# A three-block network in fp32-like products: value projections 512 features wide, and the modulations' partition sums on column tiles

## The chip, the cores and the metric

The kernel runs on one core of one Trainium2 chip. The metric is device time of one execution in microseconds (us); lower is better. A core has five engines with a queue each: TensorE for matrix products (PE in the profile, its weight loads PEld), VectorE (DVE), ScalarE (ACT), GpSimd (POOL) and SyncE (SP), which here only issues transfers. Each executes its own queue in order, and semaphores join them. A change counts here as faster or slower if it moves the time by over 0.5%.

## The reference

One sequence of 512 tokens with 1024 features goes through three blocks, here 0, 1 and 2. Each block is modulated: a vector `c` gives six vectors of 1024 numbers (shift, scale and gate for its two halves), that is 12 groups of 512 columns.

```
c_act = silu(c)
mod = c_act @ w_ada[l] + b_ada[l]
sh1, sc1, g1, sh2, sc2, g2 = split(mod, 6)
h = rms_norm(x, norm1_g[l]) * (1.0 + sc1) + sh1
x = x + g1 * mixer(h, ...)
h2 = rms_norm(x, norm2_g[l]) * (1.0 + sc2) + sh2
gate, up = split(h2 @ w_ffn_in[l], 2)
x = x + g2 * ((silu(gate) * up) @ w_ffn_out[l])
```

Block 0's mixer is dilated attention next to a gated delta rule. The mixer of the other two merges three bidirectional gated linear attentions (a, b, c) of four heads each. Every attention has a value projection `h @ w` of 512 tokens by 512 features: one in block 0 (va), three in each other block (cv, av, bv), seven in all.

## The kernel before

`T` = 512 tokens, `P` = 128 partitions, `KT` = 8 tiles of 128 features. The normed input `h` lies with features on partitions, as a high and a low part (`hh`, `hl`, in fp32r), and so does each strip of weights (`whi`, `wlo`): a product is three matmuls, high by high, high by low, low by high (`mm3`, lines 119 to 123). `strip` (104) loads 512 KB of weights on SP's queue into `raw` (2 buffers), casts it on ACT to `whi` (line 101) and subtracts on DVE to `wlo` (line 102; 3 buffers of each), with a raised priority so that it runs ahead. Most projections (`proj`, 125) hold a weight tile fixed and let 512 tokens move: 24 matmuls into one PSUM bank.

The value projections are the other way round, `proj_tok` (183): tokens must come out on partitions, so a 128x128 tile of `h` is held fixed and weights move. A call does 256 of the 512 features, with two strips of 512 rows by 256 columns held through the call. For each of 4 token tiles it issues 8 x 3 matmuls that move 256 columns (lines 193 to 195), 96 in all, into half a bank; two banks of tag `mm` hold the result. Two calls make one projection, so there are 14 calls and 1344 such matmuls. `dst` then takes both banks: a copy on ACT for va, a split on ACT and DVE for cv and av (lines 101 and 102), and for bv a copy, a mean and a subtraction first (1201 to 1207). PSUM has 3 banks of tag `mm` (projections) and 5 of tag `mx` (everything else).

The modulations are not matrix products. `ada` (283) multiplies 128 x 512 tiles of `w_ada` by a column of `c_act` and adds them up on DVE into `acc` (305, 307). What is left, the sum over 128 partitions, is `ada_sum` (317), one group of 512 columns at a time. Block 0 (`li` = 0; groups 4 to 11, during the first mixer) does it with one fp32 matmul against a column of ones, which the profile records as two passes. Blocks 1 and 2 (all 12 groups, during the feed-forward of the block ahead) first split `acc` on ACT and DVE and then use two fp32r matmuls. Both are line 325. A sum is traced where the next group begins. The row is scaled on ACT (326), written to DRAM (327), read back (332) and transposed (340). Block 0's `acc` has two buffers, and its weight tiles (`araw`) two buffers of 256 KB.

`Dense` holds such work as a list of items with a cost each. The chains of the mixers call `fill(us)` at every step, which issues items until their cost is covered; `proj_tok`'s items are 2 x 5.2 us each, before the change. In the mixers the chain `c_decay` (1223), then `scan` (1067) with its copies `kt` (1085) and small matmuls (1104, 1123), is traced ahead of the value projection that fills its waits. The framework's scheduler orders each engine's queue at build time, by priority (the order of tracing, unless raised) and its own estimate of durations, and inserts every wait; a tile takes any free buffer of its tag. The modulations of block 0's first norm, which the change doesn't touch, already put fp32 matmuls of 32 columns on four column tiles (`ada_first`, line 387).

## Time and profile before

| what | value |
|---|---|
| median of 3 runs | 2854.15 us (2843.81 to 2860.08) |
| the profiled execution, span | 2841.0 us |
| PE busy | 2774.7 us (98%), 17518 matmuls |
| PEld busy | 2234.6 us (79%) |
| DVE busy | 1721.8 us (61%) |
| ACT busy | 1172.0 us (41%) |
| transfers | 330.66 MB, mean 116 GB/s |
| mean granted TensorE clock | 0.994 |

The span runs from the first to the last instruction of the profiled execution, which lies 13 us below the median of the runs and 3 us below the fastest. Matmuls are pipelined: a record lasts from its start to a modelled end and overlaps the next one, so what a matmul costs is read from one start to the next, not from its duration. A granted clock of 1.00 is 2.4 GHz, 0.50 is 1.2 GHz.

### The profile page before, as it was taken

What the parts mean: (1) busy time and instruction counts of PE and PEld (TensorE: products, weight loads), DVE (VectorE), ACT (ScalarE), POOL (GpSimd) and SP (SyncE); (2) the same over time, 40 slices, a digit from 0 to 9 for tenths busy, and PEclk for the clock granted to TensorE, in tenths of its full rate; (3) what the DMA queues carried; (4) which work ended last, traced back from release to release, by engine and by line L of the source; (5) the groups of instructions that cost most, each with busy time, mean ns of one, the idle gap of its engine ahead of it and who ended that gap; (6) DMA issues with size and microseconds to landing.
All of it is one profiled execution on the core that took longest, in us unless ns stands there. A gap on an engine that the chain in (4) does not pass through costs nothing.

```text
span 2841.0 us, 42612 instructions
## 1 busy us (share of the span) xinstructions
PE 2774.7 (98%) x17518; PEld 2234.6 (79%) x17518; DVE 1721.8 (61%) x2690; ACT 1172.0 (41%) x1796; POOL 41.7 (1%) x79
## 2 busy tenths in 40 slices
PE   7999999999999999999999999999999999999998
PEld 4786678878888887787887888877877888888887
DVE  4677646747377767756466563567777665533334
ACT  4643324222255655444343222465454443422223
POOL 0011000000000000100000000000000000000000
PEclk9999999999999999999999999999999999999999
DMA  7454524646232222332446463322223324333332
GB/s 259 126 157 117 156 87 144 228 150 215 84 110 62 68 72 68 101 93 83 133 134 210 153 224 93 103 66 68 68 75 90 99 80 130 89 97 96 92 94 82
DMA packets 471315, 330.66 MB, mean 116 GB/s; under 512 B 15447, under 2 KB 426223, under 8 KB 469584
## 3 DMA queue, kind: packets, MB, share of 16 engines
q1 hardware_dynamic: 468176, 320.51, 37.2%
q0 software_dynamic: 2944, 7.43, 0.9%
q8 instruction: 138, 2.26, 0.3%
q14 instruction: 57, 0.47, 0.1%
HBM read 312.55 MB, written 13.24 MB: 115 GB/s over the span
## 4 chain that ended last, share of the span: by engine, by line
PE 89%; DVE 4%; ACT 3%; DMA 2%; issue 1%; SPq 1%; POOL 0%; ACTq 0%; DVEq 0%; POOLq 0%
PE mm L121 22%; PE mm L122 22%; PE mm L123 22%; PE mx L121 3%; PE mx L122 3%; PE mx L123 3%; PE mm L193 1%; PE mm L195 1%; PE mm L194 1%; PE mx L1104 1%; PE mx L1123 1%; ACT whi L101 1%; PE mx L325 1%; PE mx L940 1%; DVE R L1154 1%
## 5 line engine op out<-in xcount | busy, mean ns | idle before, releaser
L121 PE MATMUL mm<-hh,whi 128*128 128x512 f32 (+1 forms) x2248 | 873.0, 391 | 12.4 <-ACT hh L487 9.0
L122 PE MATMUL mm<-hl,whi 128*128 128x512 f32 (+1 forms) x2248 | 876.9, 391 | 2.5 <-DVE hl L488 1.8
L101 ACT CAST whi<-raw 128x1024 fp32r<-128x1024 f32 (+2 forms) x451 | 438.3, 973 | 1068.6 <-PE mm L122 737.9
L123 PE MATMUL mm<-hh,wlo 128*128 128x512 f32 (+1 forms) x2248 | 874.0, 390 | 0.0
L102 DVE TENSOR_TENSOR wlo<-raw,whi 128x1024 fp32r<-128x1024 f32 (+2 forms) x451 | 507.4, 1126 | 361.5 <-ACT whi L101 350.0
L121 PEld LDWEIGHTS mm<-hh,whi 128*128 128x128 f32 x2248 | 419.6, 188 | 113.6 <-ACT hh L487 12.0
L122 PEld LDWEIGHTS mm<-hl,whi 128*128 128x128 f32 x2248 | 422.6, 188 | 102.5 <-DVE hl L488 6.0
L123 PEld LDWEIGHTS mm<-hh,wlo 128*128 128x128 f32 x2248 | 422.5, 188 | 93.4 <-issue 0.8
L122 PE MATMUL mm<-hid,whi 128*128 128x512 f32 (+1 forms) x564 | 212.7, 377 | 0.0
L121 PE MATMUL mm<-hid,whi 128*128 128x512 f32 (+1 forms) x564 | 212.5, 377 | 0.0
L123 PE MATMUL mm<-hid,wlo 128*128 128x512 f32 (+1 forms) x564 | 212.1, 376 | 0.0
L492 DVE SCALAR_TENSOR_TENSOR x<-mm,mod,x 128x512 f32<-128x512 f32 (+1 forms) x116 | 80.4, 694 | 180.6 <-PE mm L123 180.3
L307 DVE SCALAR_TENSOR_TENSOR acc<-araw,cs,acc 128x512 f32<-128x512 f32 x224 | 167.9, 750 | 17.6 <-DMA araw<-in_w_ada_dram 12.9
L542 DVE TENSOR_TENSOR sg<-mm,sg 128x512 f32<-128x512 f32 x66 | 45.6, 691 | 159.5 <-PE mm L123 158.0
L1154 DVE TENSOR_TENSOR R<-R,tot 128x512 f32<-128x512 f32 x192 | 126.0, 685 | 12.5 <-PE mx L1123 10.9
L193 PE MATMUL mm<-whi,hh 128*128 128x256 f32 x448 | 128.7, 287 | 2.0 <-ACT q_all L663 2.0
L195 PE MATMUL mm<-whi,hl 128*128 128x256 f32 x448 | 128.3, 286 | 0.0
L194 PE MATMUL mm<-wlo,hh 128*128 128x256 f32 x448 | 127.7, 285 | 0.0
L121 PEld LDWEIGHTS mm<-hid,whi 128*128 128x128 f32 x564 | 106.2, 188 | 20.4 <-issue 0.8
L122 PEld LDWEIGHTS mm<-hid,whi 128*128 128x128 f32 x564 | 106.2, 188 | 19.2
L123 PEld LDWEIGHTS mm<-hid,wlo 128*128 128x128 f32 x564 | 106.2, 188 | 19.1
L193 PEld LDWEIGHTS mm<-whi,hh 128*128 128x128 f32 x448 | 85.2, 190 | 4.3 <-ACT q_all L663 2.5
(384 smaller groups left out, 3507.2 us busy)
## 6 DMA issues: line engine op xcount, KB each, us to landing
raw<-in_w_in_dram SPq DMA_DIRECT2D x164, 512.0 KB
araw<-in_w_ada_dram SPq DMA_DIRECT2D x48, 1024.0 KB
raw<-in_w_ffn_in_dram SPq DMA_DIRECT2D x88, 512.0 KB
araw<-in_w_ada_dram SPq DMA_DIRECT2D x64, 256.0 KB
raw<-in_w_ffn_out_dram SPq DMA_DIRECT2D x32, 512.0 KB
raw<-in_w_gate_dram SPq DMA_DIRECT2D x22, 512.0 KB
raw<-in_w_up_dram SPq DMA_DIRECT2D x22, 512.0 KB
raw<-in_w_ada_dram SPq DMA_DIRECT2D x16, 512.0 KB
```

The lines of the kernel that those rows point to most:

```text
L101: self.nc.scalar.copy(out=hi, in_=src)
L102: self.nc.vector.tensor_tensor(out=lo, in0=src, in1=hi.bitcast(F32), op=ALU.subtract)
L121: m(out=ps, lhsT=w[0], rhs=a[0], start=first, stop=False)
L122: m(out=ps, lhsT=w[0], rhs=a[1], start=False, stop=False)
L123: return m(out=ps, lhsT=w[1], rhs=a[0], start=False, stop=last)
L193: m(out=o, lhsT=a[0][:, sl], rhs=hi[:, k % 4], start=k == 0, stop=False)
L194: m(out=o, lhsT=a[0][:, sl], rhs=lo[:, k % 4], start=False, stop=False)
L195: m(out=o, lhsT=a[1][:, sl], rhs=hi[:, k % 4], start=False, stop=k == KT - 1)
L307: nc.vector.scalar_tensor_tensor(out=acc, in0=raw, scalar=cs[:, k:k + 1], in1=acc, op0=ALU.mult, op1=ALU.add)
L492: self.nc.vector.scalar_tensor_tensor(out=self.x(f)[:, sl], in0=ps[:, sl], scalar=g[:, f:f + 1], in1=self.x(f)[:, sl], op0=ALU.mult, op1=A ...
L542: nc.vector.tensor_tensor(out=sg, in0=pu, in1=sg, op=ALU.mult)
L1154: v.tensor_tensor(out=o, in0=o, in1=half(1 - c), op=ALU.mult)
```

## The change

A value projection becomes a generator of four steps. Each step loads one strip of 256 rows by all 512 columns and, for each of the 4 token tiles, issues 2 x 3 matmuls that move 512 columns, into a whole bank per token tile: three `mm` banks and one `mx` bank, which accumulate over the four steps. The last step hands each bank to `dst` as soon as that token tile is done. The items in the lists become four of 5.2 instead of two of 10.4.

The modulations' sums are collected: four groups at a time for blocks 1 and 2 (their accumulators are the four rows of one tile `accs`), two for block 0. `ada_sum` then issues one plain fp32 matmul per group, against a column of ones read 32 times, on the column tile 32 j of one `mx` bank, one ACT copy for all, and one DMA per group. The split into high and low parts is gone. Blocks 1 and 2 read all their rows back once, at the end, where they did it in two halves.

```diff
     def proj_tok(self, w, act, dst):
-        ps = [self.mm(), self.mm()]
-        W = [self.strip(w[half * 512:(half + 1) * 512], 4, 256) for half in range(2)]
         m = self.nc.tensor.matmul
-        for tt in range(4):
-            o = ps[tt // 2][:, (tt % 2) * 256:(tt % 2) * 256 + 256]
-            sl = slice(tt * P, tt * P + P)
-            for k in range(KT):
-                a, (hi, lo) = act(k), W[k // 4]
-                m(out=o, lhsT=a[0][:, sl], rhs=hi[:, k % 4], start=k == 0, stop=False)
-                m(out=o, lhsT=a[0][:, sl], rhs=lo[:, k % 4], start=False, stop=False)
-                m(out=o, lhsT=a[1][:, sl], rhs=hi[:, k % 4], start=False, stop=k == KT - 1)
-        for b in range(2):
-            dst(b, ps[b].rearrange("p (t f) -> p t f", t=2))
+        ps = []
+        for i in range(4):
+            hi, lo = self.strip(w[i * 256:(i + 1) * 256], 2, T)
+            ps = ps or [self.mm(), self.mm(), self.mm(), self.mx()]
+            for tt in range(4):
+                sl = slice(tt * P, tt * P + P)
+                for k in range(2):
+                    a = act(2 * i + k)
+                    m(out=ps[tt], lhsT=a[0][:, sl], rhs=hi[:, k], start=i + k == 0, stop=False)
+                    m(out=ps[tt], lhsT=a[0][:, sl], rhs=lo[:, k], start=False, stop=False)
+                    m(out=ps[tt], lhsT=a[1][:, sl], rhs=hi[:, k], start=False, stop=i == 3 and k == 1)
+                if i == 3:
+                    dst(tt, ps[tt])
+            yield
...
     def ada(self, li, g, part):
+        most = 4 if li else 2
         if part == 0:
-            if self.sums:
+            if len(self.sums) == most:
                 self.ada_sum()
-            self.acc = self.wp.tile([P, T], F32, name="acc", tag="acc", bufs=2)
+            if li == 0:
+                self.acc = self.wp.tile([P, T], F32, name="acc", tag="acc", bufs=2)
+            else:
+                if not self.sums:
+                    self.accs = self.t8("accs")
+                self.acc = self.accs[:, len(self.sums)]
...
-            parts = [acc]
-            if li:
-                t = self.t8("ada", F32R)
-                parts = [t[:, 0], t[:, 1]]
-                self.split(parts[0], parts[1], acc)
-            self.sums.append((li, g, parts))
+            self.sums.append((li, g, acc))
 
     def ada_sum(self):
-        li, g, parts = self.sums.pop()
+        if not self.sums:
+            return
         ps = self.mx()
         row = self.t2("row")
-        ones = self.mean128[:, 0:1] if li else self.mean
-        for i, a in enumerate(parts):
-            nc.tensor.matmul(out=ps[0:1], lhsT=ones, rhs=a, start=i == 0, stop=i == len(parts) - 1)
-        nc.scalar.mul(out=row[0:1], in_=ps[0:1], mul=float(P if li else D))
-        nc.sync.dma_start(out=self.mods[li][g:g + 1], in_=row[0:1])
+        n = len(self.sums)
+        for j, (li, g, acc) in enumerate(self.sums):
+            nc.tensor.matmul(out=ps[32 * j:32 * j + 32], lhsT=cap(self.one, 0, [[0, 32]]), rhs=acc, start=True, stop=True,
+                             tile_position=(0, 32 * j))
+        nc.scalar.copy(out=row[:32 * n], in_=ps[:32 * n])
+        for j, (li, g, acc) in enumerate(self.sums):
+            nc.sync.dma_start(out=self.mods[li][g:g + 1], in_=row[32 * j:32 * j + 1])
+        self.sums = []
...
-        for half in range(2):
-            d.add("va", 2 * C, lambda half=half: va_in(half))
+        for _ in range(4):
+            d.add("va", C, lambda: next(va_in))
...
-                self.split(to[0], to[1], ps)
-            self.proj_tok(W[:, c0 + 256 * half:c0 + 256 * half + 256], H, dst)
+                self.split(hi[:, tt], lo[:, tt], ps)
+            yield from self.proj_tok(W[:, c0:c0 + T], H, dst)
+
+        def tok_in(name, c0):
+            steps = tok(name, c0)
+            for _ in range(4):
+                d.add(name, C, lambda: next(steps))
...
-                if g == 3 and i == 0:
-                    d.add("gate", 0.4, lambda: self.ada_rows(li, groups[0], 3))
-            if g in (2, 5):
+                if li == 0 and g == 3 and i == 0:
+                    d.add("gate", 0.4, lambda: self.ada_rows(li, 2, 3))
+            if li == 0 and g == 2 or g == 5:
+                g0 = 0 if li else max(g - 2, groups[0])
                 d.add("ada", 0.4, self.ada_sum)
-                d.add("ada", 0.4, lambda g0=max(g - 2, groups[0]), g1=g + 1: self.ada_load(li, g0, g1))
-        d.add("ada", 0.4, lambda: self.ada_rows(li, 3, 6))
+                d.add("ada", 0.4, lambda g0=g0, g1=g + 1: self.ada_load(li, g0, g1))
+        d.add("ada", 0.4, lambda: self.ada_rows(li, 0 if li else 3, 6))
```

## Rows read from the trace of the kernel before

**Rows 1.** The page, busy time by engine and the shares of the chain that ended last
```profile
PE 2774.7 (98%) x17518; PEld 2234.6 (79%) x17518; DVE 1721.8 (61%) x2690; ACT 1172.0 (41%) x1796; POOL 41.7 (1%) x79
PE 89%; DVE 4%; ACT 3%; DMA 2%; issue 1%; SPq 1%; POOL 0%; ACTq 0%; DVEq 0%; POOLq 0%
```
**Rows 2.** PE's waits: waiter, releaser: us in total, times, longest
```profile
PE mm L121 <- ACT hh L487: 9.0, 11, 1.5
PE mx L1104 <- ACT kt L1085: 8.2, 2, 5.5
PE mx L325 <- DVE acc L307: 6.2, 3, 3.5
```
**Rows 3.** First feed-forward: stretch, us, busy PE, PEld, DVE, ACT, POOL, clock, DMA, GB/s
```profile
520.00:820.00 300.00, 298.59 (x1333) 242.12 (x1331) 169.47 (x225) 93.60 (x127) 0.00 (x0) 1.00 0.48 154
```
**Rows 4.** One bv projection, both calls, PE alone: stretch, us, busy (matmuls), clock, DMA, GB/s
```profile
1196.95:1219.98 23.03, 23.03 (x193) 1.00 0.31 82
```
**Rows 5.** PE's timeline behind it (start, us, line, tiles): a projection of 24 wide matmuls
```profile
1219.98 0.40 PE L121 MATMUL mm<-hh,whi 128*128 128x512 f32 x1
...
1225.56 0.39 PE L121 MATMUL mm<-hh,whi 128*128 128x512 f32 x1
```
**Rows 6.** PE's timeline in the output projection, six wide matmuls apart
```profile
1410.45 0.39 PE L121 MATMUL mm<-mh,whi 128*128 128x512 f32 x1
...
1411.81 0.39 PE L121 MATMUL mm<-mh,whi 128*128 128x512 f32 x1
```
**Rows 7.** The page's groups, the narrow value products of one kind, all 14 calls
```profile
L193 PE MATMUL mm<-whi,hh 128*128 128x256 f32 x448 | 128.7, 287 | 2.0 <-ACT q_all L663 2.0
```
**Rows 8.** PE's timeline, fp32 matmuls on column tiles: two (4 passes), later four (8)
```profile
22.41 1.05 PE L387 MATMUL mx<-raw,cz 128*32 128x512 f32 x4
23.39 0.38 PE L475 MATMUL mx<-c_ident,col 128*128 128x128 f32 x1
...
47.05 0.40 PE L122 MATMUL mm<-hl,whi 128*128 128x512 f32 x1
47.38 1.06 PE L387 MATMUL mx<-raw,cz 128*32 128x512 f32 x8
48.37 0.50 PE L123 MATMUL mm<-hh,wlo 128*128 128x512 f32 x1
48.71 0.39 PE L121 MATMUL mm<-hh,whi 128*128 128x512 f32 x1
```
**Rows 9.** PE's timeline, a modulation sum of block 1, and all of blocks 1 and 2
```profile
488.77 0.63 PE L325 MATMUL mx<-ada,mean 128*1 128x512 f32 x2
489.24 0.40 PE L121 MATMUL mm<-hh,whi 128*128 128x512 f32 x1
...
L325 PE MATMUL mx<-ada,mean x48: 392/396/399, 488.8 to 1734.1; 128*1 128x512 f32 x48
```
**Rows 10.** PE's timeline, a modulation sum of block 0
```profile
372.44 1.02 PE L325 MATMUL mx<-acc,mean 128*1 128x512 f32 x2
373.39 0.50 PE L122 MATMUL mm<-ya,whi 128*128 128x512 f32 x1
```
**Rows 11.** PE's timeline at the longest wait for an accumulator, and the clock behind it
```profile
348.75 0.39 PE L123 MATMUL mm<-ya,wlo 128*128 128x512 f32 x1
352.64 1.87 PE L325 MATMUL mx<-acc,mean 128*1 128x512 f32 x2 [3.50 <-DVE acc L307]
...
352.00:358.00 6.00, 5.36 (x110) 3.68 (x112) 3.08 (x5) 2.45 (x6) 0.00 (x0) 0.50 0.78 220
```
**Rows 12.** DVE's timeline, the first product of group 10 behind the sum at 337.30
```profile
338.30 0.49 DVE L305 TENSOR_SCALAR acc<-araw,cs 128x512 f32<-128x512 f32 x1 [0.55 <-DMA araw<-in_w_ada_dram]
```
**Rows 13.** PE's timeline, block 2: the scan's wait amid cv, and the clock there
```profile
1866.58 1.01 PE L1104 MATMUL mx<-R,kt 64*32 64x32 f32 x64 [5.46 <-ACT kt L1085]
...
1864.00:1870.00 6.00, 3.42 (x75) 3.36 (x76) 4.96 (x9) 3.54 (x6) 0.00 (x0) 0.50 0.01 3
```
**Rows 14.** How av's banks are taken, by instruction: min/median/max ns
```profile
L101 ACT CAST avh<-mm x8: 579/587/592, 992.5 to 2025.3; 128x512 fp32r<-128x512 f32 x8
L102 DVE TENSOR_TENSOR avl<-mm,avh x8: 681/685/692, 994.3 to 2026.8; 128x512 fp32r<-128x512 f32 x8
```

More of the change, by code (lines that the diff above doesn't have):

```diff
@@ L887, in mixer1 @@
         qa, ka = {}, {}
-        def va_in(half):
-            def dst(b, ps):
-                nc.scalar.copy(out=va[:, 2 * b:2 * b + 2, half * 256:half * 256 + 256], in_=ps)
-            self.proj_tok(W[:, 1024 + 256 * half:1280 + 256 * half], self.hact, dst)
+        va_in = self.proj_tok(W[:, 1024:1536], self.hact, lambda tt, ps: nc.scalar.copy(out=va[:, tt], in_=ps))
         def qa_in(t):
@@ L1189, in mixer2, with tok, dst @@
         C = 5.2
-        def tok(name, c0, half):
-            if half == 0:
-                st[name] = [self.t8(name + x, F32R) for x in "hl"]
-            hi, lo = st[name]
-            cols = slice(half * 256, half * 256 + 256)
-            def dst(b, ps):
-                to = [a[:, 2 * b:2 * b + 2, cols] for a in (hi, lo)]
+        def tok(name, c0):
+            hi, lo = st[name] = [self.t8(name + x, F32R) for x in "hl"]
+            def dst(tt, ps):
                 if name == "bv":
-                    c = self.t2("bv").rearrange("p (t h f) -> p t h f", t=2, h=2)
-                    nc.scalar.copy(out=c.rearrange("p t h f -> p t (h f)"), in_=ps)
-                    m = self.tp.tile([P, 2, 2], F32, name="vm", tag="sm", bufs=2)
+                    c = self.t2("bv").rearrange("p (h f) -> p h f", h=4)
+                    nc.scalar.copy(out=c.rearrange("p h f -> p (h f)"), in_=ps)
+                    m = self.tp.tile([P, 4], F32, name="vm", tag="sm", bufs=2)
                     v.tensor_reduce(out=m, in_=c, axis=mybir.AxisListType.X, op=ALU.add)
                     v.tensor_scalar(out=m, in0=m, scalar1=1.0 / P, scalar2=None, op0=ALU.mult)
-                    v.tensor_tensor(out=c, in0=c, in1=cap(m, 0, [[2, 2], [1, 2], [0, P]]), op=ALU.subtract)
-                    ps = c.rearrange("p t h f -> p t (h f)")
-                self.split(to[0], to[1], ps)
-            self.proj_tok(W[:, c0 + 256 * half:c0 + 256 * half + 256], H, dst)
+                    v.tensor_tensor(out=c, in0=c, in1=cap(m, 0, [[1, 4], [0, P]]), op=ALU.subtract)
+                    ps = c.rearrange("p h f -> p (h f)")
+                self.split(hi[:, tt], lo[:, tt], ps)
[4 more added lines that the diff above has]
+                d.add(name, C, lambda: next(steps))
         def fm(c0):
@@ L1388, in mixer2 @@
         d.add("lr", C, lr_in)
-        for half in range(2):
-            d.add("cv", 2 * C, lambda half=half: tok("cv", 4608, half))
+        tok_in("cv", 4608)
         cgate(0)
@@ L1401, in mixer2 @@
         d.add("c1 end", 0, lambda: None)
-        for half in range(2):
-            d.add("av", 2 * C, lambda half=half: tok("av", 1536, half))
+        tok_in("av", 1536)
         for h in range(4):
@@ L1413, in mixer2 @@
             d.add(f"a{h} end", 0, lambda: None)
-        for half in range(2):
-            d.add("bv", 2 * C, lambda half=half: tok("bv", 3072, half))
+        tok_in("bv", 3072)
         for h in range(4):
```

## The prediction

> **What bounds the kernel now.** I read the page first: PE is busy 98% of the span and holds 89% of the chain that ended last [rows 1]; apart from PE's own weight loads nothing is over 61%. So a microsecond taken off PE's queue is a microsecond off the time, unless a wait takes its place. Second, PE's waits: the longest totals are 9.0, 8.2 and 6.2 us [rows 2]. The 8.2 us stand in the scans behind `c_decay`, amid the projections cv of blocks 1 and 2; the 6.2 us are modulation sums of block 0, for which DVE's accumulator came late. Both belong to work that the change touches. Third, the stretches of the feed-forward: PE is busy 298.59 of 300 us there, DVE and ACT 169 and 94 [rows 3], so what the change takes off DVE and ACT (24 splits) is hidden now and worth nothing by itself. Last, PE's timeline for what one matmul costs, from start to start.
>
> **Value projections.** Two calls of bv run with nothing between: 192 narrow matmuls in 23.03 us [rows 4], 0.120 us each. All 14 calls issue 3 x 448 = 1344 [rows 7], 161.2 us. The change issues 672 that move 512 columns. No row shows one whose moving operand is a strip. The nearest are the projections around them: 24 in 5.58 us when `hh` and `hl` move [rows 5], 0.2325 each, and 6 in 1.36 us when `mh` moves [rows 6], 0.2267 each. So 672 cost 152.3 to 156.2 us, and the gain is 5.0 to 8.9 us. What is saved is the part of a matmul that doesn't grow with its columns. Which end applies can't be told: what moves differs, by 6 ns, with no cause in sight. I take the middle, 7 us, and keep both ends.
>
> The Trainium skill speaks against a gain of this size: TensorE: Matmul & The Clock Gate, section Back-to-back issue gap, gives a matmul N / 2.4 + 2.5 ns, so two narrow ones would cost only 2.5 ns more than a wide one, and 672 times that is an estimate of 1.7 us. The trace disagrees: 0.120 us for 256 columns is 13 ns above 256 / 2.4 [rows 4]. The forecast goes by the rows; the rule's result is a rival below.
>
> Strips stay 4 to a projection, of 512 KB, with the same casts; each now serves 24 matmuls, as in every other projection, so prefetching doesn't get tighter. Their DMAs stay on SP at the same places. The evacuation is the same eight operations, 0.59 us on ACT and 0.69 on DVE for a bank [rows 14], but comes in one run at the end of the fourth step. The wait it adds: all three `mm` banks are held from the first step to the last, where one was free before, so the next projection can't start until the first bank is read. That bank's last product lies 18 matmuls, 18 x 0.23 = 4.1 us, ahead of the next projection; its read takes 0.59 + 0.69 = 1.3 us plus what stands in ACT's and DVE's queues. Behind a late read would stand PE's whole queue. I cost it at nothing, covered by those 4.1 us; it is the slower rival. One `mx` bank of five goes to the fourth token tile for that time; the scan works in two banks at a time at most places, so I take nothing for it. Items of 5.2 instead of 10.4 keep the sum of costs, so what follows in the lists is reached at about the same step; in the first mixer two more list steps start block 0's modulations a little earlier, which costs nothing.
>
> **Sums of blocks 1 and 2.** Removed: 24 pairs of fp32r matmuls (x48), a pair from 488.77 to 489.24 [rows 9], 0.47 us, 11.3 us in all. Added: six batches of four fp32 matmuls on four column tiles. The trace has just this form: 8 passes from 47.38 to the next start at 48.37, 0.99 us, with 0.33 us to the start ahead and 0.34 behind where a wide matmul takes 0.23 [rows 8], so about 1.2 us with both turns. 6 x 1.2 = 7.2; the gain is 4.1 us (5.3 if the turns cost nothing). Each batch ends in one ACT copy of a bank and four small DMAs on SP in a row where four came apart; a strip queued behind them waits for that copy some 2 us at most, under the 5.58 us that one strip's matmuls last [rows 5]. Dropping the half-way read-back and its transpose is worth under 1 us; the last one stays where it was.
>
> **Sums of block 0.** Removed: 8 fp32 matmuls of two passes, from 372.44 to 373.39 [rows 10], 0.95 us. Added: 4 batches of two on two column tiles, 22.41 to 23.39 [rows 8], 0.98 us. The turns stand on both sides, 0.2 us each. 8 x 1.15 - 4 x 1.18 = 4.5 us, or 3.7 without turns; I take 4.
>
> The batches stand where every second sum stood. Group 10's sum goes, and it is the one on which PE waited longest: 3.50 us at 352.64, and then at half clock, 0.50 from 352 to 358, where the sum itself takes 1.87 us instead of 1.02 [rows 10, 11]. What is next there are the chunk products of the delta rule (839), whose operands are ready; behind them stand strips whose `wlo` shares DVE's queue with the products that wait for `araw`'s transfers. So between nothing and about 6 us come back; I take 3.5. The other sums that waited stay. A new wait: both accumulators are in use until a batch has run, so DVE's first product of the next group waits for PE, and `wlo` and residual steps behind it. The trace has that order already: at 338.30 that product started 1.0 us after its predecessor's sum, for its transfer [rows 12]. I cost it at nothing.
>
> **The scans behind cv.** PE waits 5.46 us for `kt` in block 2, and the clock is at 0.50 from 1864 to 1870 [rows 13]; block 1's wait is the rest of 8.2 [rows 2]. The wait comes from a queue order that puts the scan's matmuls ahead of value products that were ready. The change deals that order anew. The chain that sets the wait is untouched, so I take zero; the bounds are -9 us (both waits gone, half of a slow stretch of 6 us regained, less what moves elsewhere) and +5.
>
> **The sum.** 7 + 4 + 4 + 3.5 = 18.5 us off the span of 2841.0: 2822.5. The median shown is 13 us above the span, and I apply the same difference: 2854.15 - 18.5 = 2835.7, forecast 2836. The ends of the costs alone: 8.9 + 5.3 + 4.5 + 6 + 9 = 33.7 below, 5.0 + 4.1 + 3.7 + 0 - 5 = 7.8 below: 2820 to 2846.
>
> **Rivals.** First, the matmuls save what they should and the waits eat some of it: the 3.5 us turn up at the next accumulator, because `araw`'s transfers set that pace, and the scans lose 5. That is 18.5 - 3.5 - 5 = 10 us: 2844. For it: DVE waits for `araw` in the same stretch. Against: PE has some 110 matmuls next [rows 11], most of them without such an operand. 20%.
>
> Second, a wide value product costs two narrow ones less 2.5 ns, 0.2375 us, because a moving strip is slower still than moving `hh` (which is 6 ns slower than `mh`). Then 1.7 us take the place of 7: 2841. Against it: the narrow products move strips too and carry 13 ns above their columns [rows 4], as the wide ones that move `mh` do [rows 6]. 8%.
>
> Third, the column tiles don't run together, so the change doesn't do what it says: each of four matmuls takes its two passes alone, about 0.95 us [rows 10]. Then 24 x 0.95 + 1.2 = 24 us take the place of 11.3, and block 0 keeps about its 9: the two sums lose 12.5 instead of gaining 8, and 2836 + 20.5 gives 2856, no change. Against it stands the same form in [rows 8]. 6%.
>
> Fourth, slower: the held banks. At the end of each of the six value projections of blocks 1 and 2 the read of the first bank stands in ACT's or DVE's queue behind a scan's step, and PE waits. It decides from a read that comes over 4.1 us late; at 3.1 us of wait for each the gain is gone. If each waits the 5.46 us that ACT was late by in [rows 13], that is 32.8 us, and some 15 more from the slower clock behind it: 2836 + 48 = 2884. For it: cv and av are stretched through scans. Against: bv and va are not, and such a late ACT shows twice in the trace. 9%.
>
> **How the numbers follow.** The forecast has 57%. 0.5% is 14.3 us, about what a measurement of this kernel can tell from no change: the forecast's 18.5 lies beyond it, the first three rivals within it, the fourth on the other side. So faster 0.57, same 0.34, slower 0.09. The range: below, 2820; above, it takes in the first three rivals to 2856 and leaves out the fourth.
>
> **What would show it.** Right: 672 wide value matmuls at 0.227 to 0.233 us from start to start; six batches of eight passes and four of four, each about 1 us; the wait at group 10's sum gone with its slow clock; PE's busy time about 15 us less. Wrong: batches of over 2 us; starts at 0.2375; PE waiting for ACT or DVE on `mm` banks at the first matmul behind a value projection; a longer wait for `kt`.

## The result: slower, 2878 us

| what | before | after |
|---|---|---|
| median of 4 runs | 2854.1 us | 2878.1 us |
| ratio, 95% interval | | 1.0089 [1.0064, 1.0114] |
| the profiled execution, span | 2841.0 us | 2874.8 us |
| PE busy | 2774.7 us | 2788.7 us |
| clock | 0.994 | 0.983 |

The forecast was 2836 us, faster. The medians are 24 us apart the other way (25 by the ratio), beyond the range. The page of the changed kernel, with busy times and the shares of the chain that ended last, then PE's waits there (waiter, releaser: us in total, times, longest), which answer to [rows 1, 2]:

```profile
PE 2788.7 (97%) x16844; PEld 2210.1 (77%) x16844; DVE 1707.4 (59%) x2664; ACT 1154.2 (40%) x1753; POOL 41.7 (1%) x79
...
PE 86%; ACT 4%; DVE 4%; DMA 3%; issue 1%; SPq 1%; POOL 0%; ACTq 0%; DVEq 0%
```
```profile
PE mx L1110 <- ACT kt L1091: 17.3, 6, 5.4
...
PE mx L349 <- DMA mrow<-mods: 3.8, 1, 3.8
...
PE mx L331 <- DVE acc L316: 3.4, 1, 3.4
...
PE mm L121 <- ACT va L898: 2.9, 1, 2.9
```

There are 674 matmul records fewer and PE is busy 14 us more, where the prediction expected 15 less; the granted clock is lower (0.983 against 0.994). PE's share of the chain fell, and the scans' waits for `kt` went from 8.2 us in 2 to 17.3 in 6.

Where the time went is read by cutting PE's timeline at the last product of each stage (`yd` ends the first mixer, `hid` a feed-forward, `mh` the mixers of blocks 1 and 2). All runs of this study in one table, us of one profiled execution each, with the ratio to the kernel before:

| kernel | ratio [95%] | mixer 0 | FFN 0 | mixer 1 | FFN 1 | mixer 2 |
|---|---|---|---|---|---|---|
| before | 1 | 436.4 | 381.5 | 628.2 | 378.5 | 631.8 |
| after | 1.0089 [1.0064, 1.0114] | 456.4 | 378.5 | 639.3 | 378.4 | 637.5 |
| e1_sums | 1.0005 [0.9994, 1.0016] | 439.5 | 378.7 | 629.3 | 377.2 | 631.6 |
| e2_values | 1.0112 [1.0095, 1.0129] | 453.2 | 381.1 | 638.6 | 378.5 | 636.3 |
| x1_cv | 1.0056 [1.0039, 1.0073] | 436.3 | 381.4 | 640.1 | 379.8 | 636.9 |
| x2_va | 1.0062 [1.0046, 1.0078] | 454.2 | 381.0 | 629.2 | 379.8 | 632.1 |
| e7_av_bv | 0.9985 [0.9973, 0.9998] | 444.3 | 378.8 | 628.8 | 378.3 | 633.3 |
| e8_bv | 0.9987 [0.9978, 0.9995] | 438.7 | 378.8 | 628.9 | 378.0 | 633.3 |
| x4_bv_b0 | 1.0010 [0.9998, 1.0022] | 450.5 | 379.8 | 629.7 | 376.0 | 633.0 |
| x5_va_items | 1.0013 [1.0004, 1.0021] | 441.9 | 382.4 | 630.3 | 378.5 | 633.3 |
| x9_best | 1.0001 [0.9989, 1.0014] | 442.8 | 378.5 | 628.3 | 377.2 | 632.2 |
| e5_hold | 1.0005 [0.9997, 1.0014] | 438.7 | 381.3 | 629.9 | 379.8 | 632.9 |
| e3_mm4 | 1.0051 [1.0036, 1.0066] | 440.1 | 378.0 | 637.7 | 376.0 | 638.1 |
| e4_own | 1.0068 [1.0054, 1.0081] | 447.6 | 380.1 | 639.7 | 376.0 | 637.9 |
| e9_before_mm4 | 1.0075 [1.0063, 1.0087] | 457.0 | 381.6 | 630.4 | 379.8 | 633.5 |
| x3_cv_early | 1.0058 [1.0042, 1.0074] | 443.1 | 381.0 | 642.4 | 378.6 | 639.6 |
| x6_cv_pass | 1.0036 [1.0023, 1.0049] | 436.2 | 381.5 | 634.0 | 379.8 | 637.7 |
| x8_cv_items | 1.0036 [1.0023, 1.0049] | 441.0 | 382.4 | 638.0 | 379.8 | 638.4 |
| y1_cv_strips4 | 1.0079 [1.0063, 1.0094] | 457.4 | 381.5 | 639.7 | 378.6 | 634.6 |
| y2_before_strips4 | 1.0066 [1.0052, 1.0080] | 455.8 | 381.5 | 636.1 | 378.5 | 629.1 |

A ratio of 0.001 is 2.85 us. Mixer 0 is between 436.2 and 444.3 in all kernels with the first mixer of the kernel before, three buffers of strips and three `mm` banks, so a difference under 8 us there says nothing by itself. (The expectations of e1_sums to e4_own cut the stages some us elsewhere.) The two profiled spans differ by 34 us, the medians by 24, so up to 10 us of the differences between the first two rows belong to these two executions and not to the kernels. The loss is in the mixers: 20, 11 and 6 us. The feed-forwards, where only the sums changed, are 3 us shorter.

The two prices that the sum was built on came out close to what was put. One value projection alone, bv of block 1: stretch, us, busy PE, PEld, DVE, ACT, POOL, clock, DMA, GB/s; it answers to [rows 4]. Then PE's timeline around a batch of four sums, which answers to [rows 8, 9]:

```profile
1225.70:1248.10 22.40, 22.40 (x97) 18.02 (x96) 17.30 (x23) 8.78 (x12) 1.96 (x4) 1.00 0.40 105
```
```profile
569.31 0.39 PE L123 MATMUL mm<-hid,wlo 128*128 128x512 f32 x1
569.62 1.06 PE L331 MATMUL mx<-accs,one 128*32 128x512 f32 x8
570.62 0.50 PE L121 MATMUL mm<-hid,whi 128*128 128x512 f32 x1
570.96 0.39 PE L122 MATMUL mm<-hid,whi 128*128 128x512 f32 x1
```

96 wide products from 1225.70 to the next start at 1248.10 are 22.40 us, 0.2333 each, where the 192 narrow ones of such a projection took 23.03. The batch takes 1.00 us with 0.31 and 0.34 at its turns.

### The profile page after: what moved, and what is told of

Read it like the earlier page. It is cut to its first block, busy times and chain, and to the rows that moved or that the text cites. A ratio compares the mean times of both kernels' runs of the same rounds, so it can differ in the third digit from the quotient of the medians.

```text
span 2874.8 us, 41181 instructions
## 1 busy us (share of the span) xinstructions
PE 2788.7 (97%) x16844; PEld 2210.1 (77%) x16844; DVE 1707.4 (59%) x2664; ACT 1154.2 (40%) x1753; POOL 41.7 (1%) x79
## 4 chain that ended last, share of the span: by engine, by line
PE 86%; ACT 4%; DVE 4%; DMA 3%; issue 1%; SPq 1%; POOL 0%; ACTq 0%; DVEq 0%
PE mm L121 22%; PE mm L122 22%; PE mm L123 22%; PE mx L121 3%; PE mx L122 3%; PE mx L123 3%; DMA araw<-in_w_ada_dram 2%; PE mx L1110 1%; ACT whi L101 1%; PE mm L195 1%; PE mm L196 1%; PE mm L197 1%; DVE wlo L102 1%; PE mx L1129 1%; PE mx L946 1%
## 5 line engine op out<-in xcount | busy, mean ns | idle before, releaser
L316 DVE SCALAR_TENSOR_TENSOR accs<-araw,cs,accs 128x512 f32<-128x512 f32 x168 | 125.6, 750 | 5.2 <-DMA araw<-in_w_ada_dram 1.0
L455 DVE RECIPROCAL rstd<-rstd 128x512 f32<-128x512 f32 x24 | 80.4, 3351 | 13.6 <-ACT rstd L454 13.6
L121 PE MATMUL mx<-y,whi 128*128 128x512 f32 x192 | 75.7, 394 | 0.0
L122 PE MATMUL mx<-y,whi 128*128 128x512 f32 x192 | 75.5, 393 | 0.0
L123 PE MATMUL mx<-y,wlo 128*128 128x512 f32 x192 | 75.2, 392 | 0.0
```

What stands on the lines that cost most here:

```text
L121: m(out=ps, lhsT=w[0], rhs=a[0], start=first, stop=False)
L122: m(out=ps, lhsT=w[0], rhs=a[1], start=False, stop=False)
L123: return m(out=ps, lhsT=w[1], rhs=a[0], start=False, stop=last)
L316: nc.vector.scalar_tensor_tensor(out=acc, in0=raw, scalar=cs[:, k:k + 1], in1=acc, op0=ALU.mult, op1=ALU.add)
L455: nc.vector.reciprocal(out=r, in_=r)
```

## Experiments: which part loses

**Sums alone, and value projections alone.** e1_sums is the kernel before with the changed `ada`, `ada_sum` and their list; e2_values is the changed kernel with the old ones, that is the two parts of the diff ahead of the prediction, one each.

```diff
+        most = 4 if li else 2                       # e1_sums: with the rest of that part
...
+            ps = ps or [self.mm(), self.mm(), self.mm(), self.mx()]      # e2_values: with the rest of that part
```

> The kernel before with the modulations' sums of the changed kernel (batches on column tiles); the value projections stay narrow. Between the kernel before and the changed one, the first mixer became 20 us longer (439.9 to 459.9 up to the first feed-forward), the mixers of blocks 1 and 2 became 11.0 and 5.6 longer, and the feed-forwards together 2.9 shorter. Theory: the mixers of blocks 1 and 2 (17 us) suffer from the value projections alone, so here both stay at 626.5 and 631.2, within 2, and the feed-forwards give back 3 to 5. For the first mixer two causes are open. If block 0's batches cause its 20 us (they wait for two accumulators and hold them, and the gate's read-back comes behind them), this run is at 2854 - 4 + 20 = 2870. If va causes them, the batches save what I predicted, and this run is at 2854 - 8 = 2846. The rival that the sums do nothing good anywhere gives 2854 or more with feed-forwards unchanged.

> The changed kernel with the sums of the kernel before: one group at a time. Value projections 512 wide over three mm banks and one mx bank. Theory: the 17 us of the mixers of blocks 1 and 2 are all here, since TensorE's queue around the scan behind cv is the changed kernel's (39 value products, a scan level, 11, then three levels in a row with none between them); the feed-forwards are the kernel before's. If va causes the first mixer's 20 us: 2878 + 4 = 2882. If the batches do: 2878 + 4 - 20 = 2862. The rival of my prediction (the held mm banks) would show here as waits at the first matmul behind each value projection, 3 us or more in each.

The sums alone change nothing measurable (1.0005), the value projections alone cost 32 us. Nearly all of the mixers' loss is theirs. The parts don't simply add: with the sums batched as well, the changed kernel is at 1.0089 where e2_values is at 1.0112, though these two intervals overlap.

**One projection at a time.** From the kernel before, `proj_tok` of the changed kernel (here `proj_wide`) for the projections named; e7 and e8 also have the batched sums of blocks 1 and 2.

```diff
-        for half in range(2):
-            d.add("cv", 2 * C, lambda half=half: tok("cv", 4608, half))
+        tok_in("cv", 4608)          # x1_cv; the same for va: x2_va; bv: e8_bv; av and bv: e7_av_bv
```

> The kernel before with one projection wide, cv in blocks 1 and 2, over three mm banks and one mx bank as in the changed kernel; va, av, bv and the sums are the kernel before's. TensorE's queue around the first scan is the changed kernel's: 39 value products, a level, 11, three levels with none between, 14. Theory (cv is where blocks 1 and 2 lose): the mixers become 10 and 5 us longer, as in the changed kernel (11.1 and 5.7), and the time is 2848 + 15 = 2863. Rival (the loss needs av or the batches too): mixers within 3 us, 2848 to 2853.

> The kernel before with one projection wide, va in block 0. Theory (va is what made the first mixer longer by 20 us in the changed kernel and by 16.8 with single sums): first mixer 445 to 455, 2848 + 15 = 2863; together with the run where cv alone is wide it makes up the 31 us of the run with all value projections wide and single sums. In the trace the last transitions of the delta rule (L825 of the changed kernel) then stand behind the transpose of the last read-back, where the kernel before has them 25 us ahead of it. Rival (chance in the order of transfers): within 5 us of 2848.

> The kernel before with av and bv wide over three mm banks and one mx bank, and with the batched sums in blocks 1 and 2 alone; va, cv and block 0's sums stay as they were. Theory (the loss sits where a projection runs amid a scan's first levels, in cv, and in va): the first mixer is the kernel before's 436.4 within 3, the scans behind cv keep the order of the kernel before, and what is left of the change pays: a wide projection alone takes 22.40 us instead of 23.03 (measured in bv of the changed kernel), so four save 2.5, the feed-forwards save 4: 2848 - 6.5 = 2841. If av loses as cv does (in the changed kernel block 1 lost another 3.5 us between cv and av): 2848. The rival that wide products cost everywhere: 2855 or more.

> As the run with av and bv wide, but av narrow too: only bv, which runs with nothing beside it, is wide, and the sums of blocks 1 and 2 are batched. Theory: 2848 - 1.3 - 4 = 2843, mixers of blocks 1 and 2 at 628.2 and 631.8 less 0.6 each. Against the run with av wide it says what av gives or costs: theory 1.3 us more here; if av loses as cv does, this run is the faster by 3 to 7.

cv costs 16 us and va 18, together 34 beside the 32 of e2_values. av and bv cost nothing; with the batched sums they give 4 us, and e7 and e8 are the only versions that beat both kernels (intervals below 1, but 0.15% in size, less than the prediction called measurable). What av adds to bv alone can't be told (mixers 1 and 2: 628.8 and 633.3 with it, 628.9 and 633.3 without). Like cv, av is dealt out between the levels of a scan: in e7_av_bv's block 1, 9, 16, 11, 11, 14 and 16 of its wide products stand ahead of, between and behind five levels from 995 to 1009 us, and PE waits at none of them. So being wide amid a scan need not cost.

**Block 0's batches.** x4_bv_b0 is e8_bv with block 0's sums two at a time (`most` 2 in place of 1).

> The run in which bv is wide and the sums of blocks 1 and 2 are batched (0.9987 of the kernel before), with block 0's sums batched too, two groups at a time. By the prediction this gives 4 us for the passes and 3.5 for the wait at group 10's sum: 2844 - 7.5 = 2837. By the run in which only the sums were changed (2850.1 against 2847.9, with feed-forwards 4 us shorter) block 0's batches cost some 6: 2850.

They cost: 1.0010 against 0.9987 is 6.6 us, where the prediction had a gain of 7.5. The same stretch of e1_sums, of x4_bv_b0 and of the kernel before (columns as above):

```profile
388.00:406.00 18.00, 16.99 (x90) 12.49 (x91) 2.45 (x5) 2.10 (x5) 0.00 (x0) 0.53 0.00 0
```
```profile
388.00:406.00 18.00, 17.20 (x90) 11.98 (x88) 2.99 (x5) 3.36 (x5) 0.00 (x0) 0.50 0.00 1
```
```profile
388.00:406.00 18.00, 17.05 (x141) 12.41 (x142) 4.62 (x9) 4.86 (x8) 0.00 (x0) 1.00 0.06 16
```

PE is as busy as before but at half the clock: 90 matmuls where there were 141. The last read-back of block 0 comes behind the last group's transfers: its transpose is at 374.9 and 380.2 us, where it was at 379.3. PE's waits for an accumulator did shrink: from 6.2 us in the kernel before [rows 2] to this in e1_sums,

```profile
PE mx L328 <- DVE acc L313: 2.0, 2, 1.6
```

and from 5.0 us in e8_bv to 2.1 in x4_bv_b0. What is lost lies behind the transpose: from there to the end of the first mixer the kernel before takes 57.1 us, e1_sums 64.6 and x4_bv_b0 70.3. The last seven `ya` products, which the kernel before has at 391.7 to 393.1, end at 373 in e1_sums; whether their place has to do with the clock was not tried.

## Experiments: why va

In block 0 every step of the list also lets the modulations issue 0.6 us of theirs (`d.extra`). Four items in place of two mean two more such steps, so the modulations' sums come earlier.

```diff
-        for _ in range(4):
-            d.add("va", C, lambda: next(va_in))
+        for _ in range(2):
+            d.add("va", 2 * C, lambda: (next(va_in), next(va_in)))
```

> As the run in which va alone is wide (2868, first mixer 454.2), but its four steps are dealt as two items of 10.4 with two steps each, as the kernel before dealt its two calls. In block 0 every list step also lets the modulations issue 0.6 us of their own items, so four items in place of two bring the modulations forward: there the second sum stands at 224.5 in place of 252.1, and in TensorE's queue all sums but the last stand ahead of the delta rule's last transitions (L819 of the kernel before), where the kernel before has two sums behind them. With two items the queue has the kernel before's order there. Theory (the number of list steps): first mixer 436 to 444, 2848 to 2853. Rival (the four held banks and their evacuation in one run): first mixer 450 or more, 2865.

The time went from 1.0062 to 1.0013: 14 of the 18 us were the number of items. (The expectations of x2_va and x5_va_items name a wrong line: what changes its place is the state step `mx<-rr,kdec`, line 839 before and 848 after, not the transitions.) PE's timeline of x2_va, four items, where L344 is a sum, L359 the read-back's transpose and L858 the state step:

```profile
367.02 1.86 PE L344 MATMUL mx<-acc,mean 128*1 128x512 f32 x2 [7.26 <-DVE acc L326]
...
372.31 0.27 PE L359 MATMUL mx<-c_ident,mrow 24*128 24x24 f32 x1 [3.43 <-DMA mrow<-mods]
372.51 3.76 PE L858 MATMUL mx<-rr,kdec 64*64 64x64 f32 x106
```

and of x5_va_items, two items:

```profile
356.59 1.02 PE L344 MATMUL mx<-acc,mean 128*1 128x512 f32 x2 [1.48 <-DVE acc L326]
357.54 2.38 PE L858 MATMUL mx<-rr,kdec 64*64 64x64 f32 x109
...
375.77 1.02 PE L344 MATMUL mx<-acc,mean 128*1 128x512 f32 x2 [0.45 <-DVE acc L326]
...
382.62 0.24 PE L359 MATMUL mx<-c_ident,mrow 24*128 24x24 f32 x1
```

With four items the queue has the last sum and the transpose ahead of the state step, so the delta rule's chain waits 7.26 us for `acc` and 3.43 for the read-back, neither of which it needs; with two, the state step runs 15 us earlier and the last sum later. The busy time of 350 to 372 us in x2_va, then in the kernel before:

```profile
350.00:372.00 22.00, 11.19 (x158) 7.14 (x158) 11.60 (x22) 3.03 (x5) 0.00 (x0) 0.77 0.47 143
```
```profile
350.00:372.00 22.00, 19.36 (x249) 14.28 (x250) 14.20 (x24) 5.64 (x12) 0.00 (x0) 0.84 0.74 238
```

The changed kernel has the same order, with a state step at 374.59 right behind the transpose:

```profile
369.50 1.04 PE L331 MATMUL mx<-acc,one 128*32 128x512 f32 x2 [3.40 <-DVE acc L316]
...
374.39 0.27 PE L349 MATMUL mx<-c_ident,mrow 24*128 24x24 f32 x1 [3.85 <-DMA mrow<-mods]
374.59 1.68 PE L848 MATMUL mx<-rr,kdec 64*64 64x64 f32 x40
```
```profile
371.00:385.00 14.00, 9.91 (x167) 8.60 (x168) 3.28 (x8) 2.76 (x8) 0.00 (x0) 0.51 0.42 152
```

That order is not enough by itself. e3_mm4 and e4_own below also deal va as four items, and there too the state step comes 0.2 us behind the transpose (at 365.86 and 367.98 us, after waits of 4.21 and 3.75), yet their first mixers take 440.1 and 447.6 us, where the kernel before with e3_mm4's banks takes 457.0. That the number of items costs 14 us with these banks is shown; that it does so through this order is argued from the rows.

x9_best puts va wide in two items on top of e7_av_bv:

> va wide in two items, av and bv wide, cv narrow, block 0's sums single, those of blocks 1 and 2 batched: all of the change that the runs so far left without harm. Each wide projection that runs without loss saves 0.64 us (22.40 against 23.03), five of them 3.2, and the feed-forwards save 4: 2848 - 7 = 2841. The rival that va wide costs in two items as well: 2855 or more.

x9_best is no faster than the kernel before. By x5_va_items (1.0013) va wide costs some 4 us in two items as well; x9_best lies 4.6 us above e7_av_bv, but their intervals overlap. What these 4 us are was not settled; in the changed kernel the first projection behind va waits 2.9 us for ACT to read va's first bank (last row of the waits above), in x5_va_items no such wait is among the long ones.

## Experiments: why cv

**Is it the held `mm` banks?** e5_hold is the kernel before with the third `mm` bank held through both calls.

```diff
+        if half == 0:
+            self.hold = self.mm()
+            m(out=self.hold[:, :256], lhsT=act(0)[0][:, :P], rhs=W[0][0][:, 0], start=True, stop=True)
...
+        if half == 1:
+            self.nc.scalar.copy(out=self.scr, in_=self.hold[:, :1])
```

> The kernel before (narrow value projections, single sums) plus one matmul of 256 columns and one ACT copy of a column for each of the seven value projections: they hold the third mm bank from the projection's first product until behind its last evacuation, so that all three mm banks are taken, as in the changed kernel; no mx bank is held, and nothing is wider. The two extras cost PE 7 x 0.12 = 0.8 us. TensorE's queue around the scan behind cv keeps the kernel before's order: 79 narrow products, a level, 22, 23, 24 and 23 between the next ones. Theory (the order in which products are dealt around the scans, not the wait for a held bank): 2848 to 2851, mixers within 2 us of the kernel before. Rival, the fourth of the prediction (held mm banks make the next projection wait): 3 us or more for each of seven projections, 2870, with waits on mm banks at the first matmul behind each.

No (1.0005): a bank that is held cost nothing here, where the queue's order stayed.

**Is it the fourth bank?** A level of the scan is a copy `kt` on ACT, 64 small matmuls on PE (L1110) and an update of `R` on DVE, each of which needs the one before. In the changed kernel, block 1, PE's timeline from the second level of the first scan, then ACT's and, in the last row, DVE's:

```profile
880.17 1.02 PE L1110 MATMUL mx<-R,kt 64*32 64x32 f32 x64 [3.84 <-ACT kt L1091]
881.12 0.79 PE L196 MATMUL mm<-wlo,hh 128*128 128x512 f32 x1
...
885.55 0.63 PE L197 MATMUL mm<-whi,hl 128*128 128x512 f32 x1
886.11 0.86 PE L1110 MATMUL mx<-R,kt 64*32 64x32 f32 x64
889.22 0.81 PE L1110 MATMUL mx<-R,kt 64*32 64x32 f32 x64 [2.26 <-ACT kt L1091]
892.27 1.01 PE L1110 MATMUL mx<-R,kt 64*32 64x32 f32 x64 [2.23 <-ACT kt L1091]
893.21 0.79 PE L195 MATMUL mx<-whi,hh 128*128 128x512 f32 x1
...
898.21 0.76 PE L1110 MATMUL mx<-R,kt 64*32 64x32 f32 x64
```
```profile
882.83 0.68 ACT L1091 COPY kt<-R 128x512 f32<-128x512 f32 x1 [2.71 <-DVE R L1160]
...
896.18 1.05 ACT L101 CAST whi<-raw 128x1024 fp32r<-128x1024 f32 x1 [3.96 <-PE mx L197]
897.13 0.62 ACT L1091 COPY kt<-R 128x512 f32<-128x512 f32 x1
...
893.53 1.28 DVE L1160 TENSOR_TENSOR R<-R,tot 128x512 f32<-128x512 f32 x2
```
```profile
880.00:887.00 7.00, 6.79 (x139) 5.09 (x139) 4.56 (x18) 0.80 (x2) 0.00 (x0) 0.55 0.01 2
889.00:897.00 8.00, 5.54 (x138) 4.58 (x139) 3.58 (x8) 1.61 (x3) 0.00 (x0) 0.57 0.01 2
```

By 886 us three strips have served the three token tiles with an `mm` bank, and nothing is left: two levels follow with PE idle 2.26 and 2.23 us. The fourth tile's bank is `mx`, of which `c_decay` and the scan, traced earlier, take theirs first; its products start at 893.21. Until they run, all three strip buffers stay in use, and the cast of the next strip (896.18, idle 3.96 us for PE's L197) stands ahead of the scan's `kt` in ACT's queue, though R was there at 894.8. Behind the waits the granted clock is at 0.55 and 0.57 (last two rows: stretch, then columns as above), and a wide product takes 0.44 us (ten starts from 881.12 to 885.55) instead of 0.23, so what fills a wait becomes longer than the wait: the second level's `kt` was copied by 883.51, and the level started at 886.11, behind 11 such products.

Three ways around that bank. e3_mm4 and e4_own are made from the changed kernel, x3_cv_early from x1_cv:

```diff
-        return self.pp.tile([P, T], F32, name=name, tag="mm", bufs=3)
+        return self.pp.tile([P, T], F32, name=name, tag="mm", bufs=4)       # e3_mm4, e9_before_mm4
...
-        return self.pp.tile([P, T], F32, name=name, tag="mx", bufs=5)
+        return self.pp.tile([P, T], F32, name=name, tag="mx", bufs=4)       # e3_mm4, e4_own, e9_before_mm4
...
-            ps = ps or [self.mm(), self.mm(), self.mm(), self.mx()]
+            ps = ps or [self.mm() for _ in range(4)]                            # e3_mm4
+            ps = ps or [self.mm(), self.mm(), self.mm(), self.own()]            # e4_own
...
+        d.step()                                                            # x3_cv_early: cv's first step
         c_decay()
```

> The changed kernel with four mm banks and four mx banks in place of three and five; the fourth token tile's accumulator comes from mm. Theory (the mx bank): in the changed kernel the fourth token tile can't start before c_decay and the scan give back an mx bank, the three other tiles' products are used up at the second scan level, and TensorE has nothing between the next levels. Here the queue has 12, 11, 13 and 11 value products between the scan's levels, as the kernel before had 22 to 24 narrow ones; so the waits for kt fall from 17.3 us to 8.2 or less, the mixers of blocks 1 and 2 come back to 626.5 and 631.2 within 3, less the 1 to 1.5 us that wide products save: 2878 - 17 = 2861. Against it stands one mx bank fewer for everything else, some us. Rival (the longer time comes from wide products and their evacuations in one run, not from the bank's tag): both mixers stay 11 and 5 us longer, and the time stays at 2878 or goes above it.

> The changed kernel with the fourth token tile's accumulator in a bank of its own, which nothing else uses; three mm banks, four mx banks. It differs from the run with four mm banks in that projections keep three banks. Theory (the mx bank): as there, 8 to 12 value products stand between the scan's levels again, the kt waits fall to 8.2 us or less, the mixers of blocks 1 and 2 come back: 2861. If four mm banks help by themselves (the three held banks of my fourth rival), this run stays above the other by what they give; if the two agree within 3 us, the held mm banks cost nothing. Rival (not the tag): 2878 or more.

> As the run in which cv alone is wide, but cv's first step is traced ahead of c_decay, so that the fourth token tile has its mx bank before c_decay takes four, with three mm and five mx banks as before. The queue then has 24 value products ahead of c_decay, 40 behind, and 11, 15, 6 and none between the scan's levels. Theory (the late mx bank): the bare levels in a row shrink from three to two at the end, the kt waits fall below the other run's, and of its 15 us some 10 come back, less what c_decay's later start costs (up to 5.6 us for 24 products, if the chain sets the pace): 2850 to 2858. Rival (cv wide costs whatever bank the fourth tile has, since the two runs with other banks kept mixers 5 to 10 us longer): 2863, no gain by this.

The order did what was expected of it in e3_mm4, whose waits for `kt` fell to 6.5 us:

```profile
PE mx L1129 <- DVE R L1160: 7.4, 4, 3.1
PE mx L1110 <- ACT kt L1091: 6.5, 2, 4.1
```

But the mixers stayed 10 and 6 us longer: the next waits (L1129, for DVE's R; 2.3 us in x1_cv) grew to 7.4, as cv's products were used up there. x3_cv_early gained nothing either: `c_decay` started 4 to 6 us later and the fill ended earlier still. So the late bank alone is not the cause that I had taken it for; filling one wait of this chain uncovered the next.

The control for the bank split is e9_before_mm4, four and four in the kernel before:

> The kernel before with four mm banks and four mx banks and nothing else changed: the control for the run in which the changed kernel had this split (1.0051 of the kernel before, against 1.0089 of the changed kernel as it is). Theory: the split alone is worth nothing, 2848 within 5, so that what it gave the changed kernel, some 12 us, it gave through the value projections' bank. Rival: the split is good or bad by itself, by 5 us or more, and then the other run's gain is read against this one.

It costs 21 us, nearly all in mixer 0, so e3_mm4's shorter time against the changed kernel is not the split's own gain. With this split the kernel with the whole change is 7 us faster than the one without it (1.0051 against 1.0075).

**Banks, items or width?** Both from x1_cv: x6_cv_pass does two token tiles at a time, wide, in two passes over the strips; x8_cv_items deals the four steps as two items.

```diff
+        for half in range(2):                                   # x6_cv_pass
+            ps = [self.mm(), self.mm()]
+            for i in range(4):
+                hi, lo = self.strip(w[i * 256:(i + 1) * 256], 2, T)
+                for b in range(2):
+                    tt = 2 * half + b
...
-            for _ in range(4):
-                d.add(name, C, lambda: next(steps))
+            for _ in range(2):
+                d.add(name, 2 * C, lambda: (next(steps), next(steps)))      # x8_cv_items
```

> As the run in which cv alone is wide (2865), but in two passes of two token tiles each, with all four strips loaded and cast again for the second pass: 96 matmuls of 512 columns as there, two mm banks held at a time and given back half-way, no mx bank, two items of 10.4. The queue has 12 value products ahead of c_decay, 43 behind, and 6, 5, 14 and 16 between the scan's levels: none is bare. Cost: four more strips for each of two projections, 1.05 us on ACT and 1.22 on DVE each, beside the scan's chain. Theory (holding four banks to the end, one of them mx, is what costs, not the width): mixers of blocks 1 and 2 within 4 us of the kernel before, 2848 to 2856. Rival (512 columns amid the scan cost whatever the banks): mixers 10 and 5 us longer, 2863 or more.

> As the run in which cv alone is wide (2865), but its four steps are dealt as two items of 10.4. The queue keeps three levels of the scan in a row with no value product between them and the fourth token tile's products behind them (39, 3, none, none, 14). Theory (the banks): nothing changes, 2861 to 2868. Rival (the number of list steps, as for va): the mixers come back, 2852 or less.

Either takes 6 of the 16 us away (1.0036), neither all; their intervals overlap that of x1_cv. x6_cv_pass deals two items as well, so its 6 us need not be the banks'. Last, a fourth strip buffer, paid for with one of 14 large tiles (128 x 2048 numbers each), for x1_cv and for the kernel before:

```diff
-N_T8 = 14
+N_T8 = 13
...
-        hi = self.wp.tile([P, 1024], F32R, name="whi", tag="whi", bufs=3)
-        lo = self.wp.tile([P, 1024], F32R, name="wlo", tag="wlo", bufs=3)
+        hi = self.wp.tile([P, 1024], F32R, name="whi", tag="whi", bufs=4)
+        lo = self.wp.tile([P, 1024], F32R, name="wlo", tag="wlo", bufs=4)
```

> As the run in which cv alone is wide (2865), with four buffers for strips in place of three, paid for with one of the 14 large tiles. In the changed kernel the fourth token tile's products wait for their mx bank; until they run, each of cv's strips stays in use, all three buffers are taken after three steps, and the cast of the next strip stands in ACT's queue ahead of the scan's copy kt (896.18 us, idle 3.96 us before it, with kt's operand there since 894.8). With four buffers the queue has 11, 11, 7, 14 and 10 value products between the scan's levels, none bare. Read against the kernel before with the same two sizes. Theory (the held strips and banks make most of cv's loss): within 5 us of that control. Rival (wide products amid the scan cost by themselves): 10 to 16 us above that control.

> The kernel before with four buffers for strips and 13 large tiles: the control for the run beside it. Theory and rival alike: it tells what one large tile less and one strip more do to the kernel by themselves; within 10 us of 2848, with the mixers of blocks 1 and 2 within 5 us of 628.2 and 631.8.

The control itself is 19 us slower than the kernel before, mostly in mixer 0. Against it cv wide costs 1.0079 - 1.0066 = 0.0013, 4 us in place of 16, and the intervals overlap. That speaks for the strips that the late tile keeps in use as the larger part. It doesn't settle it: the control's block 1 had lost 8 us already, and in the two profiled executions, of which the first is the slowest run of its kernel, mixers 1 and 2 differ by 9.

## Why the prediction was wrong

**Right, but for a little.** The wide product's price, just above the upper bound: 0.2333 us against bounds of 0.2267 and 0.2325. The gain is (161.2 - 672 x 0.2333) = 4.4 us, where I took 7 and bounded it at 5.0: the projections with `hh` in [rows 5] were the nearest row, not the middle. The second rival's 0.2375 fell. The Trainium skill's rule (TensorE: Matmul & The Clock Gate, section Back-to-back issue gap), which that section gives for an isolated matmul, gives an estimate of 512 / 2.4 + 2.5 = 215.8 ns for a wide product. The trace disagrees: 233.3 ns, 20 above 512 / 2.4. The batches in the feed-forwards: 1.00 us and its turns as in [rows 8]; the feed-forwards are 2.6 and 2.0 us shorter (means of the eight kernels with batches and the twelve without), 4.6 against 4.1.

**Wrong, the step on list items:** "two more list steps start block 0's modulations a little earlier, which costs nothing". It cost 14 us (x2_va against x5_va_items). I checked that the costs add up to the same, not what the extra steps put ahead of what in PE's queue.

**Wrong, the scans behind cv:** zero, with bounds of -9 and +5. It was +16 (x1_cv), and the waits for `kt` grew from 8.2 us to 17.3, which the prediction had named as a sign of being wrong. I wrote that "The change deals that order anew" and then bounded the result by the waits already there [rows 2, 13], with 5 us at most for new ones. The `mx` bank at nothing and "prefetching doesn't get tighter" belong here: a strip is held, as before, until the last of four token tiles has used it, but that tile's bank now comes late, and three strips wait for it.

**Wrong, block 0's sums:** -7.5 became some +6 (x4_bv_b0 against e8_bv). With the batches alone the waits for `acc` fell by some 3 to 4 us, as forecast, and the time was lost again at half clock behind them; I had bounded the term at no gain, not at a loss through the clock. In the changed kernel the last batch waits 3.40 us (369.50), which looks like the first rival (the wait moves to the next accumulator), but x2_va, with single sums and va as four items, waits 7.26 us there and x4_bv_b0 has no wait over 1.5 us for `acc`: it goes with va's items, not with the batches.

**The fourth rival** has the right sign and nearly the time (2884), but by luck, not by its mechanism: e5_hold holds the banks and loses nothing, and PE waited on an `mm` bank behind a value projection once, 2.9 us at va.

Still open: by what the number of va's items costs its 14 us, va's last 4 us, what makes up cv's loss beside the strips, and what sets the clock behind block 0's batches.

## What to carry over

In a kernel whose queues are dealt by a planner, a change of item size or of how long a buffer is held is a change of order, and here its cost was not bounded by the waits of the old order: bound it by what the chain loses if its fill is gone, or keep the dealing as it was and change one thing. Look at what fills each wait before and after: av, wide and still between the scan's levels, cost nothing; cv, whose products ran out after two levels, cost 16 us. Before widening an accumulation over more banks, list what each pending bank keeps in use (here the strips) and who queues for that.

## What the runs showed of the hardware

Half clock with little idle time: in e1_sums PE was busy 16.99 of 18 us from 388 to 406 and the granted clock was 0.53, behind a stretch (374 to 388) with 12.47 of 14 us busy at 1.00; the fall stands beside a wait of 1.61 us that ends at 389.01. In the kernel before, 17.05 of 18 us busy ran at 1.00, with a wait of 0.95 us that ends at 394.47. In these rows the busy time of a stretch doesn't tell which of the two clock levels it gets.

The clock cost as much as the waits: the changed kernel's mixers have PE idle 19 us longer (37.6 + 13.9 + 15.3 against 28.6 + 7.9 + 11.2 us between a record's end and the next start), and are 37 us longer; the other 18 us are busy time of PE, with fewer matmuls. In some kernels the clock was all of the loss. The first mixer, PE's idle time in it behind its first matmul, its busy time and the granted clock:

| kernel | us | PE idle | PE busy | clock |
|---|---|---|---|---|
| before | 436.4 | 28.6 | 404.55 | 0.98 |
| x4_bv_b0 | 450.5 | 25.8 | 421.59 | 0.93 |
| e9_before_mm4 | 457.0 | 29.4 | 424.41 | 0.93 |
| x2_va | 454.2 | 39.3 | 411.71 | 0.95 |
| after | 456.4 | 37.6 | 415.71 | 0.94 |

x4_bv_b0 and e9_before_mm4 wait no longer than the kernel before, within 1 us, and all of their 14 and 21 us are busy time at the lower clock; in x2_va and the changed kernel waits and clock share the loss. e3_mm4 (440.1 us) is at 0.96. What decided the clock in each was not found.
